# A transformer block on one core: weight splits two units ahead, other buffer slots for late tiles, and one bias load moved to GpSimd's queue

## The chip, the cores and the metric

The kernel runs on one core of a Trainium2 chip. The metric is the device time of one execution in microseconds (us). One execution was also profiled; all rows below come from it.

## What is computed

The reference is one layer of a streaming encoder on 256 tokens of width 1024, in float32:

```
ada = silu(c) @ w_ada + b_ada            (six rows of 1024: shift, scale, gate twice)
h   = rms_norm(x) * (1 + sc_m) + sh_m
q_lat, kv_lat, k_pe, u, C, B, g_attn, g_conv = split(h @ w_in)
a   = block_causal_attention(...) @ w_up_attn
c   = (B * causal_conv3(C * u)) @ w_up_conv
x   = x + g_m * ((sigmoid(g_attn) * a + sigmoid(g_conv) * c) @ w_o)
h   = rms_norm(x) * (1 + sc_f) + sh_f
x   = x + g_f * moe(h)                   (top 4 of 32 experts, router with bias)
out = rms_norm(x) * g_final
```

An expert computes `act(h @ w_gu[e] + b_gu[e]) @ w_down[e] + b_down[e]`, with `w_gu[e]` 1024 x 2048 and `w_down[e]` 1024 x 1024. The weights of all 32 experts, 403 MB of the 458 MB that move, are read once.

## The kernel before

**Two parts.** The front is everything up to the router and the gather of the first experts' tokens. The MoE part walks over the 32 experts.

**The engines' order.** The schedule is manual: each engine executes its instructions in the order in which the Python code emits them. All weight loads are issued by SyncE (SP), whose queue is in order too: a load whose target buffer isn't free yet holds back every load behind it. `load` is `nc.sync.dma_start`.

**The front's weights.** `jobs` lists 26 units of up to 1 MB, numbered here 0 to 25: 0, 1 the latents of `w_in`; 2, 3 C; 4 `w_uq`; 5 `w_ukv`; 6, 7 u; 8, 9 B; 10 to 13 the first gates; 14, 15 `w_up_conv`; 16 to 19 the other gates; 20, 21 `w_up_attn`; 22 to 25 `w_o`. A unit is loaded raw, and `split` (L345 to L349) makes two tiles of it, a high half rounded by ScalarE (L346) and the rest by VectorE (L347), after which the raw tile is given back. TensorE uses both halves (`mul3`, L335 to L337, and `proj`, L477). `unit()` hands out the next unit; before that, `ahead(k + 1 + LOOK[k])` emits the splits of all units up to k + LOOK[k]. So `LOOK` says how far ahead of its use a split stands in ScalarE's and VectorE's order. Before, it lies between 0 and 4: at unit 10 four units are split in a row, at unit 18 three.

**The ada chunks.** Between the units, 16 chunks of `w_ada` are used: eight by TensorE (L251), and eight by VectorE, which adds them up with one instruction of about 2.3 us each (L446). After the last, `ada_sum` (L453) adds the partitions on TensorE.

**The slots.** `Slots` manages 22 narrow buffers of 1 MB (8 KB per partition). `take` picks a free one, `give` returns it with a running number (`since`), and `pump` emits the next loads of the list `loads` as long as more than `spare` slots are free. The order of the list is the string of "w" (unit) and "a" (ada chunk). Before, `take` picks the slot that was given back first; once the list is empty it prefers one whose neighbour is in use.

```
i = min((not loads and self.since[(i ^ 1) % len(self.since)] is not None, c, i)
        for i, c in enumerate(self.since) if c is not None)[2]
```

**The MoE part's slots.** After the front, each pair of neighbouring narrow slots (2i, 2i + 1) becomes one of 11 wide slots of 2 MB. A wide slot can be loaded as soon as the last user of either narrow one is done; the free wide slots are taken in the order in which the later of the two was given back. The loads (`whole`, L999) follow in SP's queue right behind the front's last load. One expert takes four loads of `w_gu` and two of `w_down`, 2 MB each, 192 in all.

**The table of b_gu.** `bias_load` (L855) takes a narrow slot near the end of the front and loads `b_gu` into it with four loads of 128 KB on SP. `bias_table` converts it (ScalarE L862, GpSimd L863) for the bias matmul L1224.

**The end of the front, in TensorE's order.** Gates 0 to 3 (L477); the attention branch with units 20 and 21 (`mul3`), its input halves made by ScalarE L689 and GpSimd L690; `ada_sum` between the two; the transposes of the merged tensor (L797); the matmuls of `w_o` with units 22 to 25, first the lower half of the sum for all four outputs, then the upper half (`wo_mm`); between these the norm, the router and `gather0` (L920). Then the experts: bias (L1224), gate and up (L1072), gather (L1044), down (L1110), scatter (L1135).

Of the kernel before, what the change touches and what calls it, by code (L numbers as in the profile page):

```python
# [56 lines left out]
def block_kernel(ctx, tc, x, c, positions, w_ada, b_ada, norm_mix_g, w_in, q_norm_g, w_uq, kv_norm_g,  # L57
# [3 lines left out]
    V, S, G, TE = nc.vector, nc.scalar, nc.gpsimd, nc.tensor  # L61
    load = nc.sync.dma_start
# [11 lines left out]
    class Slots:  # L74
        def __init__(self, pool, since, size):
            self.pool, self.since, self.held, self.clock, self.spare = pool, since, {}, max(since), 0

            for i in range(len(since)):
                pool.tile([P, size], F32, name="w", tag=f"w{i}", bufs=1)

        def take(self, shape, dtype=F32):

            i = min((not loads and self.since[(i ^ 1) % len(self.since)] is not None, c, i)
                    for i, c in enumerate(self.since) if c is not None)[2]
            self.since[i] = None
            t = self.pool.tile([P] + list(shape), dtype, name="w", tag=f"w{i}", bufs=1)
            self.held[id(t)] = (t, i)
            return t
# [7 lines left out]
        def pump(self):  # L96
            while loads and sum(c is not None for c in self.since) > self.spare:
                loads.pop(0)()

    loads = []  # L100

    def need(ready):

        while not ready():
            loads.pop(0)()

    early = ctx.enter_context(ExitStack())
    narrow = Slots(early.enter_context(tc.tile_pool(name="narrow", bufs=1)), [0] * (2 * WIDE), 2048)
# [85 lines left out]
    with tc.tile_pool(name="front", bufs=1) as fr, \  # L194
# [148 lines left out]
        def split(raw, shape):  # L343
            hi = slot(shape, F32R)
            lo = slot(shape, F32R)  # L345
            S.activation(hi, raw, AF.Copy)  # L346
            V.tensor_tensor(lo, raw, hi, op=ALU.subtract)  # L347
            give(raw)
            return [hi, lo]  # L349
# [22 lines left out]
        def ada_load(g, j):  # L372
            def issue():
                w = slot([2048])
                load(w, ap_of(w_ada, g * 2048 + j * 6 * D, [[8 * 6 * D, P], [1, 2048]]))
                ada_raw.append((g, j, w))
            return issue

        def raw_load(shape, src):
            def issue():  # L380
                w = slot(shape)
                load(w, src)
                raws.append((w, shape))
            return issue


        units, chunks = [raw_load(*j) for j in jobs], [ada_load(*j) for j in ada_todo]
        loads += [(chunks if c == "a" else units).pop(0) for c in "wwwwwwwwwaaawwawwwwaaaawwwaawaawwwawawaaww"]
        narrow.spare = 9

        def ahead(n):
            while len(done) < min(n, len(jobs)):
                need(lambda: len(raws) > len(done))
                done.append(split(*raws[len(done)]))


        LOOK = [2, 2, 4, 3, 4, 1, 2, 0, 2, 0, 4, 1, 1, 0, 2, 2, 2, 1, 3, 3, 3, 0, 0, 0, 0, 0]

        def unit():
            k = taken[0]  # L400
            taken[0] += 1
            ahead(k + 1 + LOOK[k])
            pump()
            return done[k]
# [92 lines left out]

        pl = two()
        u = unit()
        proj(u, pl, 0, 416)  # L500
        proj(unit(), pl, 1, 416)
        ahead(5)
        qq = slot([NT, H, DQK])
# [22 lines left out]

        pc_ = twoT()
        projT(unit(), pc_, 0)
        projT(unit(), pc_, 1)

# [319 lines left out]
        def bias_load():  # L850
            raw = slot([2, 512])
            rows = b_gu.rearrange("o e (q f) -> (o e q) f", f=512)
            for t in range(2):
                for k in range(2):
                    load(raw[64 * k:64 * k + 64, t, :], rows[64 * t:64 * t + 64, :])  # L855
            raw_t[0] = raw

        def bias_table():
# [79 lines left out]
        for h in range(2):  # L938
            spread_row(p[64 * h:64 * h + 64, :], 2, 2 + h)
        S.activation(gfx, p, AF.Copy)  # L940
        bias_load()
        wo_mm(0, 1, 4, 8)
        x1_half(0, 1)
# [143 lines left out]
    def act(pg):  # L1087
        ga = mo.tile([P, 512], F32, name="ga", bufs=1)
        sgm = mo.tile([P, 512], F32, name="sgm", bufs=1)
        V.tensor_scalar(ga, pg[:, 0, :], LIMIT, None, op0=ALU.min)  # L1090
        S.activation(sgm, ga, AF.Sigmoid, scale=ALPHA)  # L1091
        V.tensor_scalar(pg[:, 1, :], pg[:, 1, :], LIMIT, -LIMIT, op0=ALU.min, op1=ALU.max)
        V.tensor_mul(ga, ga, sgm)
        V.scalar_tensor_tensor(sgm, pg[:, 1, :], 1.0, ga, op0=ALU.add, op1=ALU.mult)
        return sgm
# [122 lines left out]
    for e in range(NE):  # L1218
# [31 lines left out]
        a = act(pg)  # L1250
# [136 lines left out]
```

## Time and profile before

| | |
|---|---|
| median of 3 runs | 1178.86 us (1177.23 to 1180.64) |
| profiled execution, its own time | 1177.89 us |
| its span, first to last instruction | 1176.2 us |
| TensorE matmuls busy | 1073.2 us (91%) |
| VectorE, ScalarE, GpSimd busy | 360.1, 152.0, 36.7 us |
| DMA | 457.66 MB, mean 389 GB/s |
| mean granted TensorE clock | 0.971 |

How to read it: the profile's page divides the span into 40 equal slices of 29.4 us; a digit is the busy share of a slice in tenths. TensorE's busy time includes matmuls that run at the lower clock. The time of 1177.89 us is the span and 1.7 us around it. "SPq" is SyncE's queue, in which loads are issued; the time from a load's issue to its landing includes the time in which it stands behind earlier loads.

### The profile page before, as it was taken

How to read it: one execution, taken by the hardware profiler on the slowest of the kernel's cores; microseconds unless marked ns; L12 is line 12 of the kernel's file. 1: busy time of each engine (PE TensorE's matmuls, PEld its weight loads, DVE VectorE, ACT ScalarE, POOL GpSimd, SP SyncE). 2: the span in 40 equal slices, each digit the busy share in tenths (PEclk: the TensorE clock that was granted, in tenths of full speed). 3: DMA queues.
4: the chain of work that ended last, by engine and by line, in shares of the span. 5: the costliest groups of instructions: out<-in, count | busy, mean ns of one | idle time of the engine just before them, and what ended most of it. 6: DMA issues, size and time to landing. Idle time of an engine off the chain costs nothing. (4 is left out here: it accounts for less than half of the span.)

```text
span 1176.2 us, 11805 instructions
## 1 busy us (share of the span) xinstructions
PE 1073.2 (91%) x4914; PEld 492.1 (42%) x4914; DVE 360.1 (31%) x703; ACT 152.0 (13%) x261; POOL 36.7 (3%) x85
## 2 busy tenths in 40 slices
PE   5898997999999999999999879999888988898996
PEld 1887775753343343323433234334223422342333
DVE  3857588423221222111212112131212121211123
ACT  1545642211000010000000000000000000000001
POOL 1000003100000000000000000000000000000000
PEclk9899998979999999998999989999999999998998
DMA  9983853899999999999999999999999999999995
GB/s 362 354 286 116 316 210 146 359 428 428 428 428 428 428 426 417 427 429 427 428 427 428 427 426 428 427 427 427 428 427 427 428 427 427 427 428 428 427 420 180
DMA packets 48206, 457.66 MB, mean 389 GB/s; under 512 B 4939, under 2 KB 10088, under 8 KB 20756
## 3 DMA queue, kind: packets, MB, share of 16 engines
q1 hardware_dynamic: 47394, 456.58, 93.1%
q8 instruction: 41, 0.67, 0.2%
q10 hardware_dynamic: 674, 0.14, 0.1%
q0 software_dynamic: 80, 0.14, 0.0%
q14 instruction: 17, 0.14, 0.0%
HBM read 455.79 MB, written 1.05 MB: 388 GB/s over the span
## 5 line engine op out<-in xcount | busy, mean ns | idle before, releaser
L1072 PE MATMUL pg<-w,hsel 128*64 128x512 f32 x2048 | 458.6, 601 | 28.1 <-DMA w<-in_w_gu 28.0
L1072 PEld LDWEIGHTS pg<-w,hsel 128*64 128x64 f32 x2048 | 142.9, 138 | 328.1 <-issue 273.8
L1110 PE MATMUL pm<-w,aT 128*64 128x512 f32 (+1 forms) x1056 | 227.8, 582 | 12.1 <-DMA w<-in_w_down 10.5
L1090 DVE TENSOR_SCALAR ga<-pg 128x512 f32<-128x512 f32 x32 | 22.1, 691 | 463.3 <-PE pg L1072 447.1
L1110 PEld LDWEIGHTS pm<-w,aT 128*64 128x64 f32 x1056 | 74.3, 137 | 160.8 <-issue 133.3
L1091 ACT ACTIVATE sgm<-ga 128x512 f32<-128x512 f32 x32 | 20.2, 630 | 689.4 <-DVE ga L1090 689.4
L1116 DVE TENSOR_TENSOR yp<-gfx,pm 64x512 f32<-64x512 f32 x62 | 42.5, 685 | 199.9 <-PE pm L1110 199.4
L1044 PE MATMUL pm<-oh,xs 128*128 128x256 f32 (+1 forms) x256 | 58.6, 389 | 5.0 <-DVE oh L1031 5.0
L477 PE MATMUL mm<-w 128*128 128x512 f32 (+1 forms) x240 | 58.5, 404 | 3.0 <-ACT w L417 3.0
L347 DVE TENSOR_TENSOR w<-w 128x2048 fp32r<-128x2048 f32 (+3 forms) x26 | 57.2, 2235 | 8.3 <-ACT w L346 8.1
L1044 PEld LDWEIGHTS pm<-oh,xs 128*128 128x128 f32 x256 | 50.5, 204 | 16.6 <-issue 11.5
L335 PE MATMUL mm<-w 128*128 128x256 f32 (+1 forms) x160 | 54.9, 343 | 1.7 <-ACT w L689 1.2
L1135 PE MATMUL mm<-yp,s 128*128 128x512 f32 x120 | 54.9, 600 | 0.8 <-DVE yp L1116 0.8
L337 PE MATMUL mm<-w 128*128 128x256 f32 (+1 forms) x160 | 53.5, 334 | 2.1 <-POOL w L690 2.0
L336 PE MATMUL mm<-w 128*128 128x256 f32 (+1 forms) x160 | 53.2, 332 | 0.0
L477 PEld LDWEIGHTS mm<-w 128*128 128x128 f32 x240 | 47.8, 200 | 11.8 <-ACT w L417 3.9
L346 ACT ACTIVATE w<-w 128x2048 fp32r<-128x2048 f32 (+3 forms) x26 | 46.3, 1838 | 11.9 <-DMA w<-in_w_in 11.9
L335 PEld LDWEIGHTS mm<-w 128*128 128x128 f32 x160 | 31.0, 194 | 8.9 <-issue 3.9
L1135 PEld LDWEIGHTS mm<-yp,s 128*128 128x128 f32 x120 | 22.1, 190 | 29.9 <-issue 27.5
L1221 POOL CAST sel<-id 128x256 fp32r<-128x256 f32 x32 | 12.7, 402 | 684.0 <-PE pg L1224 683.9
L337 PEld LDWEIGHTS mm<-w 128*128 128x128 f32 x160 | 31.1, 194 | 6.2 <-POOL w L690 2.4
L251 PE MATMUL pa<-w,cact 128*32 128x512 f32 x128 | 22.1, 775 | 12.5 <-DVE rs_v L142 8.4
(282 smaller groups left out, 626.5 us busy)
## 6 DMA issues: line engine op xcount, KB each, us to landing
w<-in_w_gu SPq DMA_DIRECT2D x128, 2048.0 KB, 39.1
w<-in_w_down SPq DMA_DIRECT2D x62, 2048.0 KB, 39.1
w<-in_w_ada SPq DMA_DIRECT2D x24, 1024.0 KB, 5.8
w<-in_w_in SPq DMA_DIRECT2D x14, 1024.0 KB, 9.4
w<-in_w_o SPq DMA_DIRECT2D x4, 1024.0 KB, 7.0
w<-in_w_up_conv SPq DMA_DIRECT2D x2, 1024.0 KB
w<-in_w_up_attn SPq DMA_DIRECT2D x2, 1024.0 KB, 7.2
w<-in_w_down SPq DMA_DIRECT2D x4, 512.0 KB, 32.3
```

Of the source, the lines that this page charges most:

```text
L251: TE.matmul(pa[32 * b:32 * b + 32, :], cact[:, j:j + 1].to_broadcast([P, 32]), w[:, b * 512:(b + 1) * 512], start=(j == 0), stop=(j == 7), ...
L335: TE.matmul(o, l[0], r[0], start=start, stop=False, skip_group_check=True)
L336: TE.matmul(o, l[0], r[1], start=False, stop=False, skip_group_check=True)
L337: TE.matmul(o, l[1], r[0], start=False, stop=stop, skip_group_check=True)
L346: S.activation(hi, raw, AF.Copy)
L347: V.tensor_tensor(lo, raw, hi, op=ALU.subtract)
L477: TE.matmul(ps[i][:, :n], hT[l][:, 4 * half + q, i * P:(i + 1) * P], u[r][:, q, :], start=(half == 0 and q == 0 and l == 0 and r == 0), st ...
L1044: TE.matmul(p[:, q, :], xs[:, i, fcols(2 * q2 + q)], oh[:, i, :n], start=(i == 0), stop=(i == NT - 1))
L1072: TE.matmul(pg[64 * g:64 * g + 64, n, :], hs[k // 4][:, k % 4, c0:c0 + CAP], w[:, f0:f0 + 512], start=False, stop=(k == NQ - 1), skip_grou ...
L1110: TE.matmul(py[64 * h:64 * h + 64, :], aT[:, qa, 64 * g:64 * g + 64], w[:, h], start=(b == 0), stop=(b == 7), skip_group_check=True)
L1116: V.tensor_mul(yp[64 * k2:64 * k2 + 64, h * 512:(h + 1) * 512], gfx[hp, :], py[hp, :])
L1135: TE.matmul(acc[i][h], s2[:n, i * P:(i + 1) * P], yp[:n, h * 512:(h + 1) * 512], start=start, stop=False, skip_group_check=True)
```

## The change

Splits are emitted two units ahead of the use (three at units 2 and 3), mostly one per unit; the list of loads interleaves units and ada chunks more finely; `spare` falls from 8 to 4 in steps instead of standing at 9; from unit 10 on, `take` prefers the first sixteen narrow slots; and `b_gu` is loaded through GpSimd's queue.

```diff
@@ class Slots
             self.pool, self.since, self.held, self.clock, self.spare = pool, since, {}, max(since), 0
+            self.upto = len(since)
...
-            i = min((not loads and self.since[(i ^ 1) % len(self.since)] is not None, c, i)
-                    for i, c in enumerate(self.since) if c is not None)[2]
+            i = min((i >= self.upto, c, i) for i, c in enumerate(self.since) if c is not None)[2]
@@ the list of loads
-        loads += [(chunks if c == "a" else units).pop(0) for c in "wwwwwwwwwaaawwawwwwaaaawwwaawaawwwawawaaww"]
-        narrow.spare = 9
+        loads += [(chunks if c == "a" else units).pop(0) for c in "wwwwwwwwwaawawawwawawawawwaawawawawawaawww"]
+        narrow.spare = 8
@@ unit()
-        LOOK = [2, 2, 4, 3, 4, 1, 2, 0, 2, 0, 4, 1, 1, 0, 2, 2, 2, 1, 3, 3, 3, 0, 0, 0, 0, 0]
+        LOOK = [2, 2, 3, 3, 2, 2, 2, 2, 2, 2, 2, 2, 2, 2, 2, 2, 2, 2, 2, 2, 2, 0, 0, 0, 0, 0]
         def unit():
             k = taken[0]
             taken[0] += 1
+            narrow.spare = {4: 7, 8: 6, 14: 5, 18: 4}.get(k, narrow.spare)
+            if k == 10:
+                narrow.upto = 16
             ahead(k + 1 + LOOK[k])
@@ bias_load
-                    load(raw[64 * k:64 * k + 64, t, :], rows[64 * t:64 * t + 64, :])
+                    G.dma_start(raw[64 * k:64 * k + 64, t, :], rows[64 * t:64 * t + 64, :])
```

## Rows read from the trace of the kernel before

**Rows 1.** The page: GB/s moved in 40 equal slices of the span.

```profile
GB/s 362 354 286 116 316 210 146 359 428 428 428 428 428 428 426 417 427 429 427 428 427 428 427 426 428 427 427 427 428 427 427 428 427 427 427 428 428 427 420 180
```

**Rows 2.** Busy time by stretch; last three columns: granted clock, DMA share, GB/s.

```profile
180.00:207.00 27.00, 23.30 (x98) 17.33 (x98) 22.14 (x19) 4.90 (x5) 9.81 (x10) 0.87 0.27 102
...
212.00:242.00 30.00, 27.66 (x148) 23.31 (x146) 14.23 (x44) 10.01 (x21) 3.57 (x5) 0.88 0.99 421
242.00:420.00 178.00, 174.70 (x791) 68.18 (x792) 45.88 (x107) 13.16 (x24) 2.81 (x7) 0.98 1.01 428
420.00:670.00 250.00, 234.98 (x994) 88.21 (x994) 50.03 (x95) 10.65 (x20) 4.39 (x11) 0.97 1.01 426
670.00:1140.00 470.00, 425.04 (x1832) 159.75 (x1828) 98.35 (x193) 22.38 (x42) 6.06 (x15) 0.98 1.01 427
```

**Rows 3.** Who SyncE's queue waited for, 175 to 240 us: total, times, longest.

```profile
SPq L855 <- DVE w L729: 20.2, 1, 20.2
...
SPq L855 <- PE tp L797: 7.1, 1, 7.1
```

**Rows 4.** SyncE's issues in order of time: start, duration, line, transfer, count.

```profile
179.04 0.89 SPq L382 DMA_DIRECT2D w<-in_w_o  x2
207.22 2.48 SPq L855 DMA_DIRECT2D w<-in_b_gu  x4
209.75 20.27 SPq L999 DMA_DIRECT2D w<-in_w_gu  x8
...
229.69 0.33 SPq L999 DMA_DIRECT2D w<-in_w_gu  x1
...
250.47 0.33 SPq L999 DMA_DIRECT2D w<-in_w_gu  x1
```

**Rows 5.** Time to landing of the loads issued at 229.69, 250.47 and 172.37 us.

```profile
w<-in_w_gu SPq DMA_DIRECT2D x1, 2048.0 KB, 23.2
...
w<-in_w_gu SPq DMA_DIRECT2D x1, 2048.0 KB, 22.4
...
w<-in_w_o SPq DMA_DIRECT2D x1, 1024.0 KB, 4.8
```

**Rows 6.** TensorE's waits: 245 to 671 us, then 671 us to the end.

```profile
PE pg L1072 <- DMA w<-in_w_gu: 6.1, 6, 1.2
PE pm L1110 <- DMA w<-in_w_down: 5.0, 5, 1.3
...
PE pg L1072 <- DMA w<-in_w_gu: 21.8, 21, 1.3
PE pm L1110 <- DMA w<-in_w_down: 5.4, 5, 1.3
```

**Rows 7.** TensorE in order of time; in brackets the idle time before and its end.

```profile
177.46 0.50 PE L335 MATMUL mm<-w 128*128 128x512 f32 x1 [1.21 <-ACT w L689]
...
180.19 0.63 PE L337 MATMUL mm<-w 128*128 128x512 f32 x1 [2.00 <-POOL w L690]
...
190.27 1.62 PE L453 MATMUL pa<-w,ones 128*32 128x512 f32 x8 [3.20 <-DVE w L446]
...
213.10 0.39 PE L337 MATMUL mm<-w 128*128 128x512 f32 x1
...
229.26 0.40 PE L337 MATMUL mm<-w 128*128 128x512 f32 x1
```

**Rows 8.** VectorE, and one row of ScalarE, in order of time.

```profile
176.73 2.28 DVE L347 TENSOR_TENSOR w<-w 128x2048 fp32r<-128x2048 f32 x1
178.93 3.36 DVE L446 SCALAR_TENSOR_TENSOR w<-w,cact 128x2048 f32<-128x2048 f32 x1
182.21 3.36 DVE L347 TENSOR_TENSOR w<-w 128x2048 fp32r<-128x2048 f32 x1
185.49 4.73 DVE L446 SCALAR_TENSOR_TENSOR w<-w,cact 128x2048 f32<-128x2048 f32 x2
...
202.49 4.68 DVE L347 TENSOR_TENSOR w<-w 128x2048 fp32r<-128x2048 f32 x2 [0.94 <-ACT w L346]
...
177.83 1.90 ACT L346 ACTIVATE w<-w 128x2048 fp32r<-128x2048 f32 x1
```

**Rows 9.** A load through GpSimd (issue, landing), GpSimd's work before b_gu, and b_gu's reader.

```profile
451.23 0.72 POOL L1233 DMA_DIRECT2D w<-in_b_down  x1 [56.84 <-PE pm L1110]
...
w<-in_b_down POOLq DMA_DIRECT2D x1, 128.0 KB, 7.2
...
200.60 6.79 POOL L928 TENSOR_SCALAR rwa<-rw,a_col 128x32 f32<-128x32 f32 x8 [17.19 <-PE tp L797]
...
231.82 1.04 ACT L862 ACTIVATE bg<-w 128x1024 fp32r<-128x1024 f32 x1
```

## The prediction

> **What bounds the kernel now.** I read the page first: from the ninth slice to the 38th the DMA engines move 417 to 429 GB/s, and in the front far less, with 116 and 146 GB/s in the worst slices [rows 1]. The stretches say the same: DMA share 0.99 to 1.01 from 212 us on and 0.27 between 180 and 207 us [rows 2]. So from 212 us on the transfers are the bound. TensorE's waits confirm it: in the MoE part it waits for landings of expert weights 11.1 us before 671 us (6.1 + 5.0) and 27.2 us after it (21.8 + 5.4), in steps of about 1.2 us, so it keeps catching up with the loads [rows 6]. A change in the front is therefore worth what it adds to the stock of landed expert weights, as long as TensorE has waits left to give up.
>
> Why is the DMA idle at 180 to 207 us? SP issues the last loads of w_o at 179.04 us and nothing until 207.22 us [rows 4]. It stands at the load of b_gu and waits for that load's slot, 20.2 + 7.1 = 27.3 us [rows 3]. The expert loads stand behind it in the same queue; the first six then go out within 3 us of 209.75 us, so their slots had been free.
>
> **The change, part by part.**
>
> *b_gu leaves SP's queue.* The expert loads now wait for nothing but their own slots. Which slots these are I get by following `take` and `give` through the new order of loads, splits and drops. The 11 wide slots come free in this order: the pair used last by gate 2, the one used last by the second attention unit, two that end with the splits of units 24 and 25, two that end with the first two units of w_o, four that all end with the last matmul of w_o's fourth unit, and the one that holds raw b_gu. In the profile before, the two last splits are done at 202.49 + 4.68 = 207.17 us [rows 8] and w_o's second unit at 213.49 us [rows 7]. So six loads can be issued by 213.5 us at the latest, most of them well before. The seventh to tenth wait for 229.66 us [rows 7].
>
> *TensorE reaches that point earlier.* The attention branch has two waits that depend on the splits. Before, VectorE works between 176.73 and 190.22 us on a split, an ada chunk, a split and two ada chunks, and `ada_sum` waits 3.20 us for the last of them [rows 7, 8]. With two units of look-ahead the first of these chunks comes before the split of unit 22, about at 174.8 us, and the other split (unit 23) moves behind `ada_sum`. What is left is one split and two chunks. The split can't start before ScalarE's half ends at 177.83 + 1.90 = 179.7 us [rows 8]; with 2.4 us for the split and 4.73 us for the two chunks VectorE is done at 186.9 us instead of 190.2 us: 3.3 us earlier. TensorE must be there too: it starts the branch's second part at 180.19 us after 2.00 us for GpSimd, and VectorE, whose work beside it stretches such operations (3.36 us against 2.28 us [rows 8]), now stands idle for 2 us of that. I take 1.2 us off this wait, so TensorE ends the first unit at 185.9 us and `ada_sum` starts at about 187.0 us: **3.3 us** gained. Bounds: 0, if VectorE is no earlier, and 5.2 us, both waits whole; I take the value from VectorE's rows.
>
> *The stock of weights.* A lone 1 MB load takes 4.8 us [rows 5], of which 2.4 us are transfer at 427 GB/s, so 2.4 us go by before a load on an empty queue flows. A 2 MB load is 4.9 us of transfer. After: w_o's first two units end at 213.5 - 3.3 = 210.2 us, and the sixth load has landed by 210.2 + 2.4 + 9.8 = 222.4 us. The queue then runs empty until the four slots come free at 229.7 - 3.3 = 226.4 us; the eighth load lands at 226.4 + 2.4 + 9.8 = 238.6 us. Before, it was issued at 229.69 us and landed 23.2 us later, at 252.9 us [rows 4, 5]. The stock is **14.3 us** ahead: 11.0 us from the queue and 3.3 us from TensorE.
>
> *Does the queue stay full from there?* The tenth lands at 248.4 us; the eleventh waits for the bias table, which GpSimd finishes near 232 us; the twelfth was issued at 250.47 us, when TensorE had used the first chunk [rows 4], now 247.2 us, before the eleventh has landed (253.3 us). Before, the load issued then took 22.4 us [rows 5], that is 17 us of other loads in front; after, 14.3 - 3.3 = 11 us of these are gone and 6 us remain. TensorE frees slots faster than 4.9 us each in a gate-up, so the stock in front never gets to zero by this count.
>
> *Does it reach the end?* TensorE starts the experts 3.3 us earlier, the data stands 14.3 us earlier, so TensorE has to give up 11.0 us of waits; it has 11.1 us by 671 us and 27.2 us later [rows 6]. From about expert 14 on it is again bound by the landings, and every later landing is 14.3 us earlier, the last one and the tail behind it too.
>
> *What is costed at nothing.* The four issues on GpSimd take 4 x 0.72 = 2.9 us [rows 9], on an engine whose previous work ends at 207.4 - 3.3 = 204.1 us and whose next is the bias table. If each lands 7.2 us after its issue [rows 9], all is there by 215 us, and ScalarE reads it at 231.82 - 3.3 = 228.5 us; the cover is 13 us. One after another they would take 28.8 us, to 233 us, and ScalarE, with the transposes' copies queued behind it, would be 4.5 us late: TensorE would start the experts that much later, the queue of loads would not run dry, so the end would not move. The new order of the list and the lower `spare` only issue front loads earlier; each that I follow has landed at least 5 us before its split. Splits two ahead: three of them (17, 19 and the halves of the conv input) now wait for a slot that the unit before frees, and each is done 3 to 8 us before TensorE wants it.
>
> **Sum.** 1177.89 us (the profiled execution: span 1176.2 us and 1.7 us around it) - 14.3 = 1163.6 us. That execution lies 0.97 us under the median of the runs, so for a median I say **1164.6 us**.
>
> **Rivals.** A measurement of this kernel can tell about 0.3%, 3.5 us, from no change.
>
> *Only the issue time is saved.* If the expert loads could not go out while the front still holds its slots, because the wide tiles wait for more than their own pair, moving b_gu frees SP for the 2.5 us that its four issues take (207.22 to 209.75 us [rows 4]): 1176.4 us, no difference. Against it: the loads issued at 229.69 and 250.47 us came out one by one, each as its pair was let go, with the front still running [rows 4]. The Trainium skill ("DMA: Bandwidth & Descriptors", Issuing engines are not separate DMA queues) says that issuing from several engines saves only the sequencer's time of issue. By that rule this rival's 2.5 us is all there is; the rows show that here the queue's wait of 27.3 us goes too. Chance 0.07.
>
> *TensorE becomes the bound.* If TensorE cannot give up its waits, since the same matmuls need longer when it runs without pauses, the stock is never used up. The stretch with hardly a wait ran at a granted clock of 0.98, the later ones at 0.97 and 0.98 [rows 2], so nothing points to it. If a third of the lead came through: 1174 us, faster. Chance 0.06.
>
> *Slower: the splits come too late.* With look-ahead 2 and sixteen slots, a split on ScalarE may stand in order behind a slot that TensorE frees late, and TensorE then waits for the whole split, 1.9 + 2.3 = 4.2 us per unit [rows 8]. From unit 10 to unit 21 there are twelve. TensorE's delay moves the last matmul of w_o, and so loads seven to ten, one for one. It decides from the point where four of the twelve are exposed (16.8 us, over the 14.3 us); with six, 1164.6 + 25.2 = 1190 us. Against it: VectorE is idle a good part of 60 to 155 us, and only three splits wait for a slot. Chance 0.07.
>
> **The numbers.** Forecast 0.80; with the partial lead 0.06, faster by over 0.3% has 0.86; within it 0.07; slower 0.07. The range: without TensorE's gain the lead is 11.0 us, 1167.9 us; a split or two exposed adds a few us: up to 1170. With both waits of the attention branch gone (5.2 us) it is 16.2 us, 1162.7 us, and runs scatter by 1 to 2 us: from 1161.
>
> **What would show it.** Right: SP issues the first expert load near 173 us and six by 211 us; a gap of the DMA of about 5 us before 227 us and none later; the first expert matmul near 241.6 us; no wait for expert weights until about expert 12, the waits after 700 us as before. Wrong: a wait for a slot in SP's queue between 215 and 250 us that outlasts the transfers, TensorE waiting for L346 or L347 between 100 and 200 us, ScalarE L862 waiting for b_gu, or TensorE's waits for weights gone altogether with the end less than 8 us earlier.

## The result, and the profile after

The changed kernel takes **1166.24 us** (median of 4 runs, 1165.30 to 1166.71) where the kernel before takes 1179.32 us beside it (4 runs, 1177.23 to 1180.64): a ratio of 0.989, 95% interval 0.9873 to 0.9907. Forecast were 1164.6 us and a range of 1161 to 1170 us. The profiled execution took 1166.59 us, 11.3 us less than the profiled one of before.

Line numbers are each kernel's own. Here L345 and L346 are ScalarE's and VectorE's half of a split (before: L346, L347), L334 to L336 the matmuls of `mul3` (L335 to L337), L479 those of `proj` (L477), and L1001 the expert loads (L999).

The slices of the page, GB/s (beside [rows 1]):

```profile
GB/s 354 393 271 136 231 325 240 352 429 429 424 430 426 428 428 415 428 428 427 428 427 429 429 423 429 427 427 429 426 428 428 428 428 428 427 428 426 428 419 180
```

The stretches of the changed kernel, columns as in [rows 2] (busy time of the five engines, granted clock, DMA share, GB/s), and two stretches more:

```profile
180.00:207.00 27.00, 23.05 (x103) 17.16 (x103) 22.40 (x23) 9.18 (x8) 9.91 (x13) 0.94 0.56 209
...
212.00:242.00 30.00, 25.75 (x143) 21.75 (x142) 15.29 (x50) 10.27 (x21) 3.57 (x5) 0.88 0.98 377
242.00:420.00 178.00, 175.98 (x794) 68.37 (x796) 44.65 (x103) 13.03 (x23) 2.81 (x7) 0.98 1.01 428
...
209.00:221.00 12.00, 12.00 (x55) 8.90 (x54) 2.77 (x4) 1.49 (x5) 0.00 (x0) 1.00 1.02 345
...
224.00:231.00 7.00, 6.12 (x45) 5.54 (x43) 5.15 (x25) 4.37 (x8) 0.00 (x0) 1.00 0.93 338
```

The transfers of 180 to 207 us have doubled (102 to 209 GB/s), and from 242 us on they stand at the same 428 GB/s as before: what is won lies ahead of the experts. Between 209 and 242 us two stretches are below the full rate, 224 to 231 us with a gap (share 0.93), and 209 to 221 us without one: there the engines are busy (1.02) and yet move 345 GB/s.

Whom SyncE's queue waited for, 175 to 240 us (total, times, longest), and its issues from 172 us (start, duration from the first to the last of a group, count):

```profile
SPq L1001 <- PE mm L336: 37.6, 3, 20.6
SPq L1001 <- DVE w L346: 7.1, 2, 5.8
```

```profile
174.76 54.12 SPq L1001 DMA_DIRECT2D w<-in_w_gu  x8
228.98 1.07 SPq L1001 DMA_DIRECT2D w<-in_w_down  x2
```

The 27.3 us at L855 [rows 3] are gone. SP now waits at the expert loads themselves (L1001). The first goes out at 174.8 us instead of 209.75 us [rows 4], the next five at 197.1, 203.4, 205.5, 210.3 and 211.9 us, the seventh at 228.1 us. Time to landing of the eighth load, issued at 228.45 us, and of b_gu's four on GpSimd (median):

```profile
w<-in_w_gu SPq DMA_DIRECT2D x1, 2048.0 KB, 13.6
...
w<-in_b_gu POOLq DMA_DIRECT2D x4, 128.0 KB, 11.1
```

TensorE's waits for weights, 245 to 671 us and 671 us to the end (beside [rows 6]), and TensorE in order of time (beside [rows 7]):

```profile
PE pg L1074 <- DMA w<-in_w_gu: 2.9, 3, 1.2
PE pm L1112 <- DMA w<-in_w_down: 1.5, 2, 1.1
...
PE pg L1074 <- DMA w<-in_w_gu: 22.3, 22, 1.5
PE pm L1112 <- DMA w<-in_w_down: 6.1, 6, 1.3
```

```profile
59.94 0.39 PE L336 MATMUL mm<-w 128*128 128x256 f32 x1 [1.02 <-DVE w L346]
...
103.72 7.84 PE L479 MATMUL mm<-w 128*128 128x512 f32 x24
...
180.69 0.50 PE L336 MATMUL mm<-w 128*128 128x512 f32 x1 [0.63 <-POOL w L692]
...
188.73 1.07 PE L455 MATMUL pa<-w,ones 128*32 128x512 f32 x8 [2.76 <-DVE w L448]
...
227.65 0.40 PE L336 MATMUL mm<-w 128*128 128x512 f32 x1
...
242.00 1.19 PE L1226 MATMUL pg<-bg,sel 128*128 128x512 f32 x2 [1.28 <-DVE hsel L181]
...
631.76 3.65 PE L1112 MATMUL pm<-w,aT 128*64 128x512 f32 x16 [0.40 <-DMA w<-in_w_down]
```

The last matmul of `w_o` ends at 228.05 us (before 229.66 us [rows 7]), the experts begin at 242.0 us (before 243.8 us), and the first wait for expert weights is at 631.8 us. From there TensorE goes in step with the landings again.

### The profile page after: what moved, and what is told of

It is laid out like the page before. It is cut to its first block, busy times and chain, and to the rows that moved or that the text cites. A ratio compares the mean times of both kernels' runs of the same rounds, so it can differ in the third digit from the quotient of the medians.

```text
span 1164.9 us, 11805 instructions
## 1 busy us (share of the span) xinstructions
PE 1067.3 (92%) x4914; PEld 488.5 (42%) x4914; DVE 358.5 (31%) x703; ACT 152.8 (13%) x261; POOL 35.4 (3%) x89
## 5 line engine op out<-in xcount | busy, mean ns | idle before, releaser
L1074 PE MATMUL pg<-w,hsel 128*64 128x512 f32 x2048 | 459.4, 603 | 25.4 <-DMA w<-in_w_gu 25.2
L1093 ACT ACTIVATE sgm<-ga 128x512 f32<-128x512 f32 x32 | 20.2, 630 | 685.4 <-DVE ga L1092 685.4
L346 DVE TENSOR_TENSOR w<-w 128x2048 fp32r<-128x2048 f32 (+3 forms) x26 | 56.9, 2202 | 18.3 <-ACT w L345 18.0
L479 PE MATMUL mm<-w 128*128 128x512 f32 (+1 forms) x240 | 59.4, 408 | 2.7 <-ACT w L419 2.7
L1046 PEld LDWEIGHTS pm<-oh,xs 128*128 128x128 f32 x256 | 49.5, 200 | 15.9 <-issue 11.1
L334 PE MATMUL mm<-w 128*128 128x256 f32 (+1 forms) x160 | 54.2, 339 | 1.8 <-ACT w L691 1.2
L336 PE MATMUL mm<-w 128*128 128x256 f32 (+1 forms) x160 | 53.4, 334 | 1.7 <-DVE w L346 1.0
L479 PEld LDWEIGHTS mm<-w 128*128 128x128 f32 x240 | 48.3, 203 | 12.0 <-ACT w L419 3.8
L335 PE MATMUL mm<-w 128*128 128x256 f32 (+1 forms) x160 | 52.8, 330 | 0.0
L345 ACT ACTIVATE w<-w 128x2048 fp32r<-128x2048 f32 (+3 forms) x26 | 47.3, 1839 | 19.2 <-DMA w<-in_w_in 12.3
L334 PEld LDWEIGHTS mm<-w 128*128 128x128 f32 x160 | 30.9, 193 | 8.4 <-issue 3.5
L1103 PE MATMUL pm<-ident,sgm 128*128 128x128 f32 x128 | 23.8, 308 | 10.4 <-ACT s L1066 7.9
```

Of the source, the lines that this page charges most:

```text
L334: TE.matmul(o, l[0], r[0], start=start, stop=False, skip_group_check=True)
L335: TE.matmul(o, l[0], r[1], start=False, stop=False, skip_group_check=True)
L336: TE.matmul(o, l[1], r[0], start=False, stop=stop, skip_group_check=True)
L479: TE.matmul(ps[i][:, :n], hT[l][:, 4 * half + q, i * P:(i + 1) * P], u[r][:, q, :], start=(half == 0 and q == 0 and l == 0 and r == 0), st ...
L1046: TE.matmul(p[:, q, :], xs[:, i, fcols(2 * q2 + q)], oh[:, i, :n], start=(i == 0), stop=(i == NT - 1))
L1074: TE.matmul(pg[64 * g:64 * g + 64, n, :], hs[k // 4][:, k % 4, c0:c0 + CAP], w[:, f0:f0 + 512], start=False, stop=(k == NQ - 1), skip_grou ...
```

## The experiments

A measure for all of them is the **lead**: how much earlier than the profiled execution of before a run has moved its first 300 MB, counted from the packets in its trace. If the transfers bound the MoE part, the lead is what the end gains. It is settled early: at 90 MB, which every run has moved by 298 us, it lies within 0.3 us of its value at 300 MB. Theory A is the prediction's: the end moves by the stock of expert weights, and that is set by when the wide slots come free. Each rival stands with its experiment. Times are in us; "before" is the median in the same job, and the last column is 1177.89 us less the profiled time.

| kernel | median (range, runs) | before | ratio, 95% | lead | profiled gain |
|---|---|---|---|---|---|
| changed | 1166.24 (1165.30–1166.71, 4) | 1179.32 | 0.989 (0.9873–0.9907) | 11.2 | 11.3 |
| e1 b_gu on GpSimd alone | 1167.03 (1164.11–1168.31, 6) | 1178.24 | 0.9901 (0.9884–0.9919) | 10.1 | 9.6 |
| e2 changed, b_gu on SP | 1166.70 (1165.21–1169.41, 6) | 1178.24 | 0.9903 (0.9886–0.992) | 8.4 | 8.5 |
| e3 new LOOK and b_gu alone | 1162.81 (1162.68–1164.87, 4) | 1178.24 | 0.9872 (0.9852–0.9891) | 15.3 | 15.2 |
| e4 changed, spare 9 at first | 1167.37 (1165.31–1169.71, 6) | 1178.24 | 0.9905 (0.9888–0.9923) | 10.6 | 10.8 |
| e5 changed, b_gu on ScalarE | 1168.26 (1167.23–1171.06, 6) | 1177.12 | 0.9926 (0.9914–0.9938) | 9.0 | 9.0 |
| e6 new LOOK alone | 1173.66 (1172.43–1175.51, 5) | 1177.12 | 0.9967 (0.9954–0.998) | 2.4 | 2.4 |
| e7 e3, table made early | 1161.24 (1160.46–1162.27, 4) | 1176.58 | 0.9868 (0.9851–0.9884) | 17.3 | 16.1 |
| e8 changed again | 1165.31 (1164.54–1165.86, 4) | 1176.58 | 0.9902 (0.9886–0.9919) | 12.5 | 12.4 |
| e9 e3 again | 1161.64 (1161.45–1163.58, 4) | 1176.58 | 0.9877 (0.986–0.9893) | 16.4 | 16.2 |
| e10 changed, old choice of slots | 1164.27 (1162.05–1165.16, 5) | 1178.34 | 0.988 (0.9867–0.9893) | 14.2 | 13.7 |
| e11 e3, new choice of slots | 1167.02 (1166.31–1171.74, 6) | 1178.34 | 0.9914 (0.9898–0.993) | 11.4 | 11.6 |

In eleven of the twelve profiles the lead is the gain within 0.5 us; e7 is off by 1.2 us. The same kernel in another job had a lead 1.1 to 1.3 us greater (changed and e8, e3 and e9), so two profiles of different jobs can't be told apart below that. Most of this already stands at 31 us, where TensorE waits for an early VectorE instruction (L327 before): that wait ends at 30.99 us in the changed kernel and at 30.09 us in e8, at 31.87 us in e3 and at 30.50 us in e9.

**e1: b_gu alone.** The kernel before with

```diff
-                    load(raw[64 * k:64 * k + 64, t, :], rows[64 * t:64 * t + 64, :])
+                    G.dma_start(raw[64 * k:64 * k + 64, t, :], rows[64 * t:64 * t + 64, :])
```

> The kernel before, with b_gu alone moved to GpSimd's queue. Theory A (the end moves by the stock of expert weights, and the stock is set by how many wide slots come free before the last units of w_o end, and when the next one does): six loads out by 213 us, the seventh at 225.9 us as before, so the seventh flows from 228.3 us where before it flowed from about 241.8 us: 13.5 us, about 1165.5 us. Rival B (the gain is SP's 27 us wait for b_gu's slot): about 1166 us. Rival C (the gain comes from the order of the splits, through TensorE's front): no change, 1179 us.

1167.03 us. This one line brings nearly what the whole change brings: taking SP's wait away is enough by itself, and rival C's 1179 us is out. Theory A and rival B forecast nearly the same here; e2 parts them. Two stretches of this run:

```profile
180.00:207.00 27.00, 20.25 (x84) 14.67 (x85) 21.47 (x19) 5.87 (x5) 9.04 (x9) 0.87 0.99 413
221.00:228.00 7.00, 7.00 (x36) 5.90 (x35) 2.90 (x5) 2.15 (x7) 0.00 (x0) 1.00 0.03 14
```

Where 102 GB/s moved before, it is 413 GB/s, and then the transfers stand almost still until the seventh slot comes free.

**e2: all but b_gu.** The changed kernel with that line undone.

> The changed kernel, with b_gu back on SP's queue. Its slot there is one that ada_sum frees near 189 us, so SP stands until then and six expert loads follow from 191 us; they are landed by 226 us, and the seventh still goes out at 228 us. Theory A: the same as the changed kernel, 1166 us. Rival B: most of the gain lost, 1177 us or more. Rival C: 1166 us.

1166.70 us: b_gu's queue makes no difference to the changed kernel, and rival B's 1177 us is out. The waits of SP's queue in this run:

```profile
SPq L1001 <- PE mm L336: 20.5, 3, 15.8
SPq L857 <- DVE w L448: 14.0, 1, 14.0
...
SPq L857 <- PE pa L455: 1.6, 1, 1.6
```

b_gu's four loads (L857) still hold the queue, but for 14.0 + 1.6 us instead of 20.2 + 7.1 us, and they go out at 193.1 us instead of 207.2 us: in this kernel b_gu gets a slot that an ada chunk leaves. The new `LOOK` by itself moves that issue by only 2.3 us (e6), so most of it comes from the list, the reserve and the choice of slots; which of them was not tried. Six expert loads are out by 214.7 us, and the seventh waits for `w_o`'s last matmul as in the changed kernel. In this profile the front runs some us late from its first landings on, so that this seventh load goes out at 230.8 us (changed: 228.1) and the lead is 8.4 us. So there are two ways to the same six loads, and either is enough.

**e6: LOOK alone.** The kernel before with the new `LOOK` and nothing else.

> The kernel before with the new LOOK alone, b_gu on SP. By the book-keeping b_gu's slot is the one that unit 25's split frees near 205 us. Theory A: SP stands at b_gu until then, so expert loads start near 207 us instead of 209.75 us and flow without a gap: the gain is 2 to 4 us, 1175.5 to 1177.5 us. Rival C (the order of the splits makes the gain): about 1167 us.

1173.66 us, 3.5 us less than before in the median, with a lead of 2.4 us in the profiled execution: b_gu goes out at 204.9 us, 2.3 us earlier than before. TensorE begins the experts at 241.5 us, also 2.3 us earlier. By itself the order of the splits brings just that.

**e3: LOOK and b_gu.** The kernel before with e1's line and the new `LOOK`; the list, the reserve (`spare`) and the choice of slots stay old.

> The kernel before, with the new LOOK and b_gu on GpSimd's queue, but the old rule of take, the old list and 9 spare slots. By the book-keeping seven wide slots come free by 213 us instead of six, and the eighth near 225 us. Theory A: the eighth flows from about 228 us where before it flowed from 247 us: 17 to 18.5 us, 1160.5 to 1162.5 us. Rival B: 1166 us. Rival C: 1166 us.

1162.81 us, faster than the whole change: it seems that the parts left out cost something (e8 and e9 try it in one job). Here seven wide slots are free by 211.4 us and an eighth at 223.6 us. In the repeat (e9) two stretches read:

```profile
221.00:228.00 7.00, 6.40 (x44) 5.73 (x44) 5.24 (x22) 3.70 (x8) 0.00 (x0) 1.00 0.75 267
...
245.00:250.50 5.50, 5.50 (x28) 1.82 (x26) 0.00 (x0) 0.00 (x0) 0.00 (x0) 1.00 0.54 164
```

The first gap is the wait for the eighth slot. The second is a new limit: all eleven slots are full, and the twelfth load waits until TensorE has used the first chunk of the first expert (issue at 246.59 us). The lead of e3 falls there and just behind it from 20.9 to 15.3 us.

**e4: the reserve.** The changed kernel with `narrow.spare = 9` at first, to take away a wait of TensorE at 59.9 us.

> The changed kernel with 9 spare slots at the start instead of 8. Unit 6's split then no longer waits for the slot of raw unit 5, and TensorE should lose its 1.0 us wait near 59 us. But by the book-keeping only five wide slots come free before the last units of w_o, the sixth near 225 us. Theory A: the sixth flows from 228 us where before it flowed from 236.9 us: 8 to 9.5 us, 1169.5 to 1171 us. Rivals B and C: 1165 us, 1 us faster than the changed kernel.

1167.37 us, no difference. The wait did go, and five slots instead of six came free early, as the book-keeping said. The lead I expected was too small: the sixth load went out at 224.1 us, and I had let it flow only from 228 us. TensorE's front did get shorter. From the wait at 31 us to the end of `w_o`'s last matmul it takes 198.6 us before (31.01 to 229.66 us), 197.1 us in the changed kernel (30.99 to 228.05 us) and 195.2 us in e4 (32.47 to 227.63 us; in e9, 30.50 to 225.71 us, 195.2 us as well). The end of that wait in the three kernels, and e4's last matmul:

```profile
31.01 0.55 PE L320 MATMUL mm<-ident,w 128*128 128x128 f32 x3 [1.23 <-DVE w L327]
...
30.99 0.55 PE L319 MATMUL mm<-ident,w 128*128 128x128 f32 x3 [1.23 <-DVE w L326]
...
32.47 0.33 PE L319 MATMUL mm<-ident,w 128*128 128x128 f32 x1 [1.23 <-DVE w L326]
...
227.23 0.40 PE L336 MATMUL mm<-w 128*128 128x512 f32 x1
```

e4 started 1.5 us late and has one wide slot less early; its median isn't better.

**e5: b_gu through ScalarE's queue.** The changed kernel with

```diff
-                    G.dma_start(raw[64 * k:64 * k + 64, t, :], rows[64 * t:64 * t + 64, :])
+                    S.dma_start(raw[64 * k:64 * k + 64, t, :], rows[64 * t:64 * t + 64, :])
```

> The changed kernel with b_gu through ScalarE's queue. In the changed kernel the transfers fall to about 320 GB/s while GpSimd's b_gu flows (210 to 221 us), and the lead of the bytes falls from 15.0 to 12.7 us in it. Theory A: this was paid out of the gap before the seventh load, so the end stays: 1166 us, with a longer gap before 228 us. Rival D (the slow stretch costs): 1164 us. If ScalarE's queue holds b_gu back until it is late for its reader: TensorE starts the experts later, and the end stays.

1168.26 us, slower than both numbers. SP's waits of 195 to 240 us in this run, then b_gu's last two issues, its time to landing and the fifth expert load:

```profile
SPq L1001 <- PE mm L336: 26.3, 2, 19.3
SPq L1001 <- DMA w<-in_b_gu: 14.3, 3, 13.7
...
219.05 1.26 ACTq L857 DMA_DIRECT2D w<-in_b_gu  x2
...
w<-in_b_gu ACTq DMA_DIRECT2D x4, 128.0 KB, 3.6
...
220.60 0.33 SPq L1001 DMA_DIRECT2D w<-in_w_gu  x1
```

The fifth expert load stood until 220.6 us (in the changed kernel 210.3 us), and the trace puts that down to b_gu, which ScalarE issued from 217.9 us. It went out 0.3 us behind the end of b_gu's last issue and long before ScalarE reads b_gu, so the two don't share a slot. From 216 to 220 us the transfers stood almost still (40 GB/s). So this run didn't tell what b_gu's slow transfers through GpSimd cost; e2 tells it: without them the seventh load went out 2.7 us later than in the changed kernel and the lead is 2.8 us smaller, so no cost to the end shows.

**e8, e9: the two again, side by side.**

> The changed kernel once more, beside the other two of this job and with five rounds, so that they can be compared on one chip. Every theory: 1166.2 us again. What it tells is how far one profile scatters: the lead in bytes at the end should again be the change of the profiled time against the profile of before.

> The third experiment once more (the kernel before with splits two ahead and b_gu on GpSimd's queue alone), in the same job as the whole change. If the list of loads, the lower reserve of slots and the first sixteen slots cost something, as the third experiment against the change showed across two jobs (1162.8 against 1166.2 us), it is 3 to 4 us faster than the change here as well; if that was scatter of the jobs, the two are within 1.5 us.

1165.31 and 1161.64 us in one job: the 3.7 us are there again, so the list, the reserve or the choice of slots costs them, alone or together.

**e10, e11: which of them.** e10 is the changed kernel with the old choice,

```diff
-            i = min((i >= self.upto, c, i) for i, c in enumerate(self.since) if c is not None)[2]
+            i = min((not loads and self.since[(i ^ 1) % len(self.since)] is not None, c, i)
+                    for i, c in enumerate(self.since) if c is not None)[2]
```

and e11 is e3 with the new choice and `narrow.upto = 16` from unit 10 on.

> The changed kernel with the old choice of slots (the one given back first, and no first sixteen); the new list of loads, the lower reserve, splits two ahead and b_gu on GpSimd stay. In one job the whole change took 1165.3 us and splits and b_gu alone 1161.6 us; which of the other parts costs the 3.7 us? Book-keeping of the slots with this choice: five wide slots free by 197 us, the sixth at 211 us, the seventh not with w_o's last matmul (228 us) but with its third unit, near 223.6 us, since the pair holds halves of units 22 and 24. Theory A (what counts is when the wide slots come free): the seventh expert load is issued near 223.6 us and flows from 226 us, the eleven slots are landed only at 251 us, so that the twelfth load, issued near 248 us, finds no empty queue: lead 15 to 16.5 us, 1161.5 to 1163 us where before is 1178. Rival (the new list and the lower reserve cost it, since they move the front's loads): 1165.5 to 1166.5 us.

> The reverse: the third experiment (splits two ahead, b_gu on GpSimd's queue, old list, old reserve) with the change's choice of slots, the first sixteen from unit 10 on. Book-keeping: the first two wide slots are free long before the front's last load, a third and a fourth near 197 and 203 us, two at 211 us, and all the others with w_o's last matmul at 228 us, as in the whole change. Theory A: seventh expert load near 228 us, the transfers idle for some us before 230 us, lead 11 to 12 us, 1165 to 1167 us where before is 1178. Rival (the list and the reserve cost the 3.7 us, the choice of slots nothing): as the third experiment, 1162 to 1163 us.

1164.27 and 1167.02 us. SP's issues of the sixth, seventh and twelfth expert load in e10, then of the fifth to seventh in e11:

```profile
211.20 0.33 SPq L1003 DMA_DIRECT2D w<-in_w_gu  x1
...
223.80 0.33 SPq L1003 DMA_DIRECT2D w<-in_w_gu  x1
...
249.25 0.33 SPq L1003 DMA_DIRECT2D w<-in_w_gu  x1
```

```profile
209.94 1.91 SPq L1000 DMA_DIRECT2D w<-in_w_gu  x2
...
227.96 0.33 SPq L1000 DMA_DIRECT2D w<-in_w_gu  x1
```

The seventh load goes out at 223.80 us with the old choice and at 227.96 us with the new one, as the book-keeping said; with the new choice that is so whichever list is loaded (changed kernel 228.1 us). With the old choice the old list and reserve are better still (e9: 210.0 us), though e9's second gap takes that back. The lead at 68 MB is 15.6 us in e10 and 11.4 us in e11. So the choice of the first sixteen slots costs time: with it the seventh wide slot is free only at `w_o`'s last matmul, with the old choice at least one unit earlier. How much depends on the list. By the medians against before, e11 gains 11.3 us where e3 and e9 gain 15.4 and 14.9 us; with the new list e10 gains 14.1 us where the two runs of the changed kernel gain 13.1 and 11.3 us. What is left between e10 and e9, 0.9 us by the medians and 2.2 us by the lead, would be the list's and the reserve's; the medians are too close to show it. e10 kept 14.2 of its 15.6 us, since TensorE freed the first chunk at 249.25 us, 1.2 us later than I had taken, and the twelfth load found the queue empty. 1164.27 us lies 1.3 us above the end of what I had expected, and its interval overlaps the changed kernel's: for the new list the times by themselves don't settle it. For the old one they do: e11's interval lies above those of e3 and e9.

**e7: the last gap of e3.** The bias table is made before TensorE leaves `w_o`; only a ScalarE copy stays behind.

```diff
         def bias_table():
...
-            S.activation(bg2, raw, AF.Copy)
-            G.tensor_tensor(bg2[64:], raw[64:], bg2[64:], op=ALU.subtract)
...
+            S.activation(bg2, t2, AF.Copy)
...
+        bias_load()
...
+        bias_early()
...
-        bias_load()
```

(`bias_early`, left out here, does what has left `bias_table`, into the other half of b_gu's slot.)

> The kernel of the third experiment (old list and old choice of slots, splits two ahead, b_gu on GpSimd's queue), with the table of b_gu made early: b_gu is loaded behind the router's weights, ScalarE and GpSimd make the table's halves while TensorE is still in the last units of w_o, and one ScalarE copy is left at the old place. In the third experiment all eleven wide slots were landed at 245.3 us and the transfers stood still until TensorE had used the first chunk of the first expert at 248.0 us; on the chain to that point VectorE's L158 took 2.34 us, beside GpSimd's L863 with 2.35 us, where it takes 0.22 us alone. Theory A (the end moves by the stock of expert weights, and in that kernel TensorE's first chunk limits it): TensorE starts the experts about 2 us earlier, the twelfth load is issued near 246 us instead of 248.0 us, the lead goes from 15.3 to about 17 us: 1160.5 to 1161.5 us. Rival (the lead is settled by the slots that w_o's last matmul frees, what comes behind is made up again): as the third experiment, 1162.8 us.

1161.24 us, beside 1161.64 us of e9 in the same job: no difference that can be measured. VectorE in e9, then in e7:

```profile
229.09 2.35 DVE L158 SCALAR_TENSOR_TENSOR rs_u<-rstd,rs_v 128x1 f32<-128x1 f32 x1
```

```profile
229.40 0.22 DVE L158 SCALAR_TENSOR_TENSOR rs_u<-rstd,rs_v 128x1 f32<-128x1 f32 x1
...
231.52 0.25 DVE L892 SCALAR_TENSOR_TENSOR lg<-tp,rstd,cb 128x32 f32<-128x32 f32 x1 [1.51 <-PE tp L888]
```

The 2.1 us on VectorE went, but then it waits 1.51 us for TensorE's router matmuls: these were late next, and the experts began 0.66 us earlier (239.21 against 239.87 us), the twelfth load 0.4 us earlier. The lead is 0.9 us greater and the end isn't earlier at all. The landings show why: the lead counts all bytes moved, a landing one load's last byte, and the 46 landings recorded from the 19th expert load on lie on average 0.06 us earlier than in e9; the last one is at 1144.25 us, in e9 at 1144.24 us. So the expert loads weren't ahead. Whether the first chunk is what limits e3's end stays open.

## Why the prediction was right, and where it was not

**The sign and the mechanism: right, and shown.** The transfers bound the MoE part, and the end moved by the stock at its start: lead 11.2 us, profiled gain 11.3 us, and so in nearly every variant. Six loads before `w_o`'s last matmul, the rest behind it, a gap between: all in the forecast order (first load 174.8 us, forecast 173; six by 211.9, forecast 211). The rival by which only issue time is saved is refuted by e1: b_gu alone brought 11.2 us in the median, not 2.5. By the Trainium skill's rule ("DMA: Bandwidth & Descriptors", Issuing engines are not separate DMA queues) the time of issue is all that the move saves; the measurement differs, since the queue's wait of 27.3 us went too. The rival with splits that come too late is refuted too: only one wait for a split (L346) was added, of 1.02 us. And TensorE did give up what was needed: it starts the experts 1.8 us earlier and ends 11.3 us earlier, and of these 9.5 us its waits for weights gave 5.7 (28.0 + 10.5 us to 25.2 + 7.6 us) and shorter matmuls most of the rest (PE busy behind the first expert matmul 860.4 us to 857.2 us). The prediction took it all from the waits; why the matmuls were shorter was not followed up.

**The term "TensorE, 3.3 us": mis-sized; it measured 1.6 us** at `w_o`'s last matmul (229.66 to 228.05 us). The attention branch kept its part: POOL's wait fell from 2.00 to 0.63 us, that for the ada chunk from 3.20 to 2.76 us, and VectorE works there as I wrote, a split and two chunks:

```profile
181.63 2.40 DVE L346 TENSOR_TENSOR w<-w 128x2048 fp32r<-128x2048 f32 x1 [2.89 <-ACT w L345]
183.95 4.73 DVE L448 SCALAR_TENSOR_TENSOR w<-w,cact 128x2048 f32<-128x2048 f32 x2
```

But TensorE came to the branch 1.86 us late. The step that failed is "only three splits wait for a slot": there is a fourth, of unit 6. ScalarE's half of it waited 2.24 us for the raw slot of unit 5, and TensorE then 1.02 us at 59.9 us:

```profile
55.65 1.92 ACT L345 ACTIVATE w<-w 128x2048 fp32r<-128x2048 f32 x1 [2.24 <-DVE w L346]
```

e4 takes that wait away, and there the front to `w_o`'s last matmul is 3.5 us shorter than before: without the fourth wait, and without the next loss, the term of 3.3 us is about what comes. Another 0.9 us went in the 24 matmuls from 103.72 us on (7.84 us, before 6.92 us), behind the same short waits as before. The stretch of 101 to 108 us, before, after, and in e1:

```profile
101.00:108.00 7.00, 6.04 (x22) 0.76 0.00 0
```

```profile
101.00:108.00 7.00, 5.61 (x18) 0.53 0.37 122
```

```profile
101.00:108.00 7.00, 5.80 (x16) 0.52 0.00 0
```

The granted clock was 0.76 and is 0.53: the lower of its two levels lasted longer. In e1, which has the old splits and the old list, it was 0.52, so the change isn't shown to cause it.

**The term "queue, 11.0 us": 1.4 us too large, and come by another way.** The lead of 11.2 us less TensorE's 1.6 us leaves 9.6 us for it. I had let b_gu land 7.2 us after its issue and cost the queue nothing. It took 11.1 us in the median, and from 209 to 221 us the full queue moved 345 GB/s instead of 427: 12 us x (1 - 345 / 427) = 2.3 us of the early lead. In e2, where b_gu was not loaded at that time, the stretch has the full rate:

```profile
209.00:221.00 12.00, 12.00 (x52) 8.55 (x51) 2.27 (x4) 1.46 (x5) 0.00 (x0) 1.00 1.00 425
```

No cost to the end shows, since the six loads were done by the time the seventh could flow, and the gap took it: 4 to 5 us of gap were forecast, 7 us x (1 - 338 / 428) = 1.5 us came. The forecast gap was too long for another reason too. I let only the fifth and the sixth load flow from 210.2 us on, but by my own rows the third and the fourth wait for the last two splits, at 207.17 - 3.3 = 203.9 us (measured: 203.4 and 205.5 us). Four loads behind that are landed at 203.9 + 2.4 + 19.6 = 225.9 us and not at 222.4 us. The eighth load landed at 242.04 us, not 238.6: 1.7 us from TensorE and 1.8 us because it came 14.0 us behind the free slot and not 12.2. The two loads that came first into the empty queue took more than their 9.8 us of transfer and the 2.4 us that I took from a lone 1 MB load.

**"b_gu leaves SP's queue": only half of the cause.** I put the 11.0 us down to b_gu's queue. e1 shows that it is enough, e2 that it isn't needed: the other edits together free b_gu's slot 14 us earlier. I had followed the slots of the expert loads and not that of b_gu.

**"The new order of the list and the lower spare only issue front loads earlier": right for these, but the choice of slots wasn't free.** I named where each wide slot comes from and took it as given; against the old choice the new one keeps the seventh until `w_o`'s last matmul, and that costs 4 us with the old list (e11) and perhaps 1 to 3 us with the new one (e10). The lead came out 3 us below the forecast, the median only 1.6 us above it. The 1.3 us between are luck: I added 0.97 us for the profiled execution of before, which lay under its median, and that of the changed kernel lies 0.35 us over its own.

The fastest version tried is e3, with e7 equal to it: two of the five edits, 1161.6 us where the whole change has 1165.3 us in the same job.

## What to carry to other kernels

Where the transfers bound a long stretch, follow each buffer from its last user in the stage before to its first load: the loads' stock at the start is the gain, and an in-order queue with one late slot at its head holds up everything behind it. Before a change with several parts is priced, ask for each part what it would bring without the others: two that remove the same wait don't add up, and a third can take some back. Behind a removed limit look for the next: here the first gap (slots held by `w_o`) gave way to another (all slots full until TensorE begins).

## What the hardware showed that was not expected

A load on SP's queue was held up by loads of another queue: with b_gu on ScalarE's queue SP's fifth expert load stood 13.7 us, until 220.6 us, with b_gu as the releaser by the trace, though they share no slot; with b_gu on GpSimd's queue the same load went out at 210.3 us. The releaser is inferred by the profile, and why it was held was not tried.

Four loads of 128 KB through GpSimd's queue beside a full SP queue held the transfers at 345 GB/s for 12 us at a DMA share of 1.02; in e2, without them, the same stretch moved 425 GB/s at a share of 1.00.

A VectorE instruction on 128x1 took 2.35 us instead of 0.22 while GpSimd's subtraction for the bias table (2.35 us, the same start within 0.03 us) ran; with that moved away (e7) it took 0.22 us.
